# A pre-norm moved behind the projections: x transposed raw, the weights applied at the banks' evacuation, the row factor at the outputs

## Chip, cores, metric

One core of a Trainium2 chip. Times are device microseconds of one execution; the kernel's time is the median of its runs. TensorE is called PE (its weight loads PEld), VectorE DVE, ScalarE ACT, GpSimd POOL, and SP is the engine that issues most transfers.

## What is computed

A decoder layer in float32, 512 tokens of width 2048: RMSNorm, a sparse attention mixer with 16 heads in 4 groups, a residual, RMSNorm, a SwiGLU of width 5632, a residual, the final RMSNorm. What matters here is the first norm and who reads it:

```python
def rmsnorm(x, g):
    x32 = x.astype(jnp.float32)
    y = x32 * lax.rsqrt(jnp.mean(x32 * x32, axis=-1, keepdims=True) + RMS_EPS)
    return (y * g.astype(jnp.float32)).astype(x.dtype)
...
    proj = h @ w_in          # h = rmsnorm(x, mix_norm_g)
    q, kc, vc, ks, vs, kw, vw, gl = jnp.split(proj, bounds, axis=-1)
    q = q.reshape(Bsz, S, G, HPG, DH) * (DH ** -0.5)
    gates = jax.nn.sigmoid(gl.astype(jnp.float32)) ...
```

kc and vc are cut into 31 overlapping blocks and pass a small MLP (compressed keys and values); ks, vs serve the selected branch and kw, vw the window.

## The kernel before

**Precision.** Every float32 operand is split in a high half (a rounding copy on ACT) and a low half (a subtraction on DVE, for some weights on POOL), and each product is three matmuls: high by high, low by high, high by low (`three`, lines 272 to 274 of the kernel before).

**Weights.** A granule is 128 x 1024 elements (512 KB). `Weights` loads granules in one fixed order into three raw buffers (`raw`), splits them into four pairs `whi`, `wlo`, and hands them out: `take` gives the next one and keeps a given number split ahead. The granules in `on_pool` (0, 1 and 3 among them) get their low half on POOL, all others on DVE. `low` holds the granules that stand 48 columns into their buffer instead of at its start.

**The front.** The code is written in the order in which each engine executes it; nothing reorders it. x lies in four tiles of 128 tokens, `x0` to `x3`. The norm's weights are spread over all partitions in `gb` by a transfer. For each tile: ACT squares it with a running sum (`squares`, L374), a chain of one-column steps makes the row factor (`rstd_steps`, L217 to L228), `scaled` multiplies row factor and weights into x (three quarters on DVE, L239, one on ACT and POOL, L241 and L242), `transposed` turns it on PE into four banks (L250), and `his` and `los` write the high and low halves to `hn_h` and `hn_l` (L256, L261), laid out as 16 blocks of the width by 512 tokens.

**The first projection.** `ws(ps, i, g, c0, c1)` multiplies granule i of four (a quarter of the width) with the tokens c0 to c1. For the first 256 columns of kc the tokens are done in halves: `ws(..., 0, 256)` for the four granules, between the transposes of tiles 2 and 3, then `ws(..., 256, 512)` for all four. After it PE transposes the compression's position table (L430) and looks up the relative biases (L434).

**Afterwards.** The other projections follow. `kv_out` copies kc and vc from the bank (ACT), `build_blk` cuts the blocks, `mlp1` and `gelu` are the compression MLP, `k_out`, `q_out` and the end of `vpair` write the split keys, queries and values (`split_from`: ACT high half, DVE low half out of the bank). The attention of one head is interleaved with the projections of later heads by `pump`, a budget of PE time per step. Then come the output projection, the second norm, and the SwiGLU (tiles `f`), about 940 us to the end; there seven products stand for eight. `RESYNC` moves a tile by 32 columns in every fourteenth unit.

`hn_h` and `hn_l` have rows of 576 columns, of which 512 are used, from column 16 on in the mixer and from 0 on later.

Of the kernel before, what the change touches and what calls it, by code (L numbers as in the profile page):

```python
# [10 lines left out]
F32 = mybir.dt.float32  # L11
# [50 lines left out]
class Weights:  # L62


    def __init__(self, nc, raw, conv, specs):
        self.nc, self.raw, self.conv, self.specs = nc, raw, conv, specs
        self.nd = self.ncv = self.nt = 0
        self.r, self.c, self.place, self.on_pool, self.low, self.sums = {}, {}, {}, set(), set(), {}

# [10 lines left out]
    def split(self):  # L80
        i = self.ncv
        self.ncv += 1
        nk, ncol, _ = self.specs[i]
        if i in self.place:
            hi, lo = self.place.pop(i)
        else:
            c0 = 48 if i in self.low else 0
# [5 lines left out]
        self.nc.scalar.activation(hi[:, :n], src, AF.Copy)  # L93
        eng = self.nc.gpsimd if i in self.on_pool else self.nc.vector
        eng.tensor_tensor(lo[:, :n], src, hi[:, :n].bitcast(F32), op=OP.subtract)  # L95
# [20 lines left out]
def granules(w_in, w1k, w1v, w_out, f_in, f_out):  # L116
# [12 lines left out]

    low = set()  # L130
    out = cols(C_KC) + cols(C_KC + 256) + cols(C_VC)
# [12 lines left out]
    for g in range(G):  # L144
        out += cols(512 * g + 256)
        if g + 1 < G:
            c = 128 * (g + 1)
            out += two(C_KS + c, C_KW + c)
            low.update(range(len(out), len(out) + 4))
            out += two(C_VS + c, C_VW + c) + cols(512 * (g + 1))  # L150
    low.update(range(len(out), len(out) + 3 * N_SPILL))
    for cb in range(N_SPILL):
        out += [rows(w_out, 4 * i, 4, 256 * cb, 256) for i in range(3)]
    for cb in (2, 3):
        out += [rows(w_out, 2 * i, 2, 512 * cb, 512) for i in range(6)]
    marks = [len(out)]
    out += [rows(w_out, 12 + 2 * i, 2, 512 * cb, 512) for cb in range(4) for i in range(2)]
    for p in range(N_PLAIN):
        out += [(4, 256, [(0, 256, mat(f_in, 512 * i, 4, ffn_col(p), 256, 2 * DFF))]) for i in range(4)]
    return out, [rows(f_out, 2 * j, 2, 512 * b, 512) for b in range(4) for j in ORDER[b]], marks, low  # L160

# [7 lines left out]
def nsa_block(ctx: ExitStack, tc: tile.TileContext, x, rel_bias, mix_g, ffn_g, fin_g, w_in, w_out,  # L169
# [12 lines left out]
    psx = early.enter_context(tc.tile_pool(name="psx", bufs=2, space=PSUM))  # L182
    specs, specs2, marks, low = granules(w_in, w1k, w1v, w_out, f_in, f_out)
    W = Weights(nc, rawp, convp, specs)
    W.low = low
    W.on_pool.update((0, 1, 3))
# [119 lines left out]
    gates = keep.tile([128, NT, H, 3], F32, name="gates")  # L306
    biasc = keep.tile([128, H, 55], F32, name="biasc")
    kcc_h = keep.tile([128, G, 32], F32R, name="kcc_h")
    kcc_l = keep.tile([128, G, 32], F32R, name="kcc_l")
# [7 lines left out]
    kv_tiles(keep, 0)  # L317

    def k_out(ps, i):

        kv = [k[:, 32:].rearrange("p (t b s) -> p b t s", b=2, s=128) for k in KK[i]]
        return lambda b: split_from(ps[b].rearrange("p (t s) -> p t s", s=128), kv[0][:, b], kv[1][:, b])

# [4 lines left out]
    def q_out(ps, h0):  # L328
        def end(u):
            Q[h0 + u] = tuple(qp.tile([128, S], F32R, name=f"q{n}") for n in "hl")  # L330
            split_from(ps[u], Q[h0 + u][0], Q[h0 + u][1], SCALE)

# [3 lines left out]
    with ExitStack() as st1:  # L336
# [11 lines left out]
        with ExitStack() as st0:  # L348
            xp = st0.enter_context(tc.tile_pool(name="xp", bufs=1))
            xt = [xp.tile([128, D], F32, name=f"x{t}") for t in range(NT)]  # L350
            gb = xp.tile([128, D], F32, name="gb")
            junk = xp.tile([128, 1024], F32, name="junk")
            act(warm, epsc, AF.Sqrt)
            CUT = [(0, 1024, 1536, 2048)] + [(0, 1024, 2048)] * 3
            for t in range(NT):
                for c0, c1 in zip(CUT[t], CUT[t][1:]):
                    nc.sync.dma_start(xt[t][:, c0:c1], x[tok(t), c0:c1])
                if t:
                    W.load()
                else:  # L360
                    for i in range(2):
                        c = slice(1024 * i, 1024 * (i + 1))
                        nc.sync.dma_start(gb[:, c], mix_g[0:1, c].to_broadcast([128, 1024]))
# [3 lines left out]
            oh = xp.tile([NB + 1, UL + 16 * CL], F32, name="oh")  # L367
            dve.memset(relt[NB:NB + 1, :], NEG)
            pool.dma_start(relt[:NB, :], rel_bias)
            pool.dma_start(oh, onehot)  # L370

            def squares(t, i):
                c0, c1 = CUT[t][i:i + 2]
                act(junk[:, :c1 - c0], xt[t][:, c0:c1], AF.Square, accum_out=ss[t][:, i:i + 1])  # L374

            ss = [xp.tile([128, len(CUT[t]) - 1], F32, name=f"ss{t}") for t in range(NT)]
            ys = [xp.tile([128, 1], F32, name=f"y{t}") for t in range(NT)]
            rs = [rstd_steps(ss[t], ys[t]) for t in range(NT)]

            def trs():  # L380
                return [ps1.tile([128, 512], F32, name=n) for n in ("tr", "mlp", "tr", "mlp")]

            for i in range(3):
                squares(0, i)
            run(rs[0])
            scaled(xt[0], ys[0], gb, xt[0], 1)
            for i in range(2):
                squares(1, i)
# [4 lines left out]
            his(p0[2:], 0)  # L393
            W.split()
            p1 = transposed(xt[1], range(4), proj_tiles(4))
            los(p0, 0)
            his(p1, 1)
            for i in range(2):
                squares(2, i)
            los(p1, 1, rs[2])  # L400
            run(rs[2])
            W.split()
            squares(3, 0)
            scaled(xt[2], ys[2], gb, xt[2], 1)
            squares(3, 1)
            ps = proj_tiles()
            gs = [W.take(0)]
            run(ws(ps, 0, gs[0], 0, 256))
            p2 = transposed(xt[2], range(4), trs())
            his(p2, 2)  # L410
            los(p2, 2, rs[3])
            run(rs[3])
            W.split()
            scaled(xt[3], ys[3], gb, xt[3], 1)
            W.split()
            for i in (1, 2):
                gs.append(W.take(0))
                run(ws(ps, i, gs[i], 0, 256))
            p3 = transposed(xt[3], range(4), trs())
            his(p3, 3)  # L420
            los(p3, 3)
            gs.append(W.take(0))
            run(ws(ps, 3, gs[3], 0, 256))
            for i in range(4):
                run(ws(ps, i, gs[i], 256, 512, start=False))
                W.ahead(min(i + 1, 3))
            ps_kc0 = ps
            p = ps1.tile([128, 2, 32], F32, name="tr")
# [29 lines left out]
        def kv_out(ps, g0):  # L458
            return lambda u: act(kvT[:, g0 + u], ps[u], AF.Copy)

# [61 lines left out]
        for i in range(8):  # L522
            g = W.take()
            for t in range(NT):
# [4 lines left out]
                if i == 7:  # L529
                    act(VV[0][0][:, t], ps[t][:, :256], AF.Copy)  # L530
                    act(ge[:, t], ps[t][:, 256:304].rearrange("p (n h) -> p n h", n=3), AF.Exp, scale=-1.0)
                    dve.tensor_tensor(VV[0][1][:, t], ps[t][:, :256], VV[0][0][:, t].bitcast(F32), op=OP.subtract)
            if i == 1:
# [37 lines left out]
    with ExitStack() as st2:  # L571
# [34 lines left out]
        def vpair(g):  # L606
            ps = [p.rearrange("p (t c) -> p t c", t=2) for p in proj2()]
            for i in range(4):
                w = W.take()
                for t in range(NT):  # L610
# [8 lines left out]
                    if i == 3 and t % 2:  # L619
                        b = t // 2  # L620
                        split_from(ps[b], VV[g % 2][0][:, 2 * b:2 * b + 2], VV[g % 2][1][:, 2 * b:2 * b + 2])
            done["n"] += 1
# [186 lines left out]

    n2_hl = [t[:, :, :S] for t in hn_t]  # L810
    resid = ctx.enter_context(ExitStack())
# [23 lines left out]
    with tc.tile_pool(name="n2", bufs=1) as n2:  # L835
        act(warm, epsc, AF.Sqrt)
        gb2 = n2.tile([128, D], F32, name="gb2")
        nc.scalar.dma_start(gb2, ffn_g[0:1, :].to_broadcast([128, D]))
        xn = n2.tile([128, D + 16], F32, name="xn")
        wr_h = n2.tile([128, 6, 1024], F32R, name="wr_h")  # L840
# [545 lines left out]
```

## Time and profile before

| | us |
|---|---|
| median of 3 runs | 2196.51 |
| lowest and highest | 2192.6, 2198.13 |
| profiled execution | 2191.91 |
| its span | 2190.2 |
| PE busy | 2146.6 |

The profile is of one execution, 4.6 us under the median of the three runs. In a row of the timeline stand the start, the length, engine, line, operation, output tile <- input tiles, shapes, and in brackets the idle time before it with what ended it; the tile names of one ring of buffers have no number. A row of waits has the waiting engine and line, whom it waited for, the us in total, how often, and the longest.

### The profile page before, as it was taken

How to read it: one execution, taken by the hardware profiler on the slowest of the kernel's cores; microseconds unless marked ns; L12 is line 12 of the kernel's file. 1: busy time of each engine (PE TensorE's matmuls, PEld its weight loads, DVE VectorE, ACT ScalarE, POOL GpSimd, SP SyncE). 2: the span in 40 equal slices, each digit the busy share in tenths (PEclk: the TensorE clock that was granted, in tenths of full speed). 3: DMA queues.
4: the chain of work that ended last, by engine and by line, in shares of the span. 5: the costliest groups of instructions: out<-in, count | busy, mean ns of one | idle time of the engine just before them, and what ended most of it. 6: DMA issues, size and time to landing. Idle time of an engine off the chain costs nothing.

```text
span 2190.2 us, 37229 instructions
## 1 busy us (share of the span) xinstructions
PE 2146.6 (98%) x15154; PEld 1993.1 (91%) x15154; DVE 1564.2 (71%) x2564; ACT 935.7 (43%) x1447; POOL 121.4 (6%) x140
## 2 busy tenths in 40 slices
PE   6999999999999999999999999999999999999997
PEld 5889898888989888899999999999999888999996
DVE  5455565656645536698888888888888787877776
ACT  5343444544544324344444444344343454544344
POOL 3100000000013012000000000000000000001000
PEclk9999999999999999999999999999999999999999
DMA  5655232232263452244433333443334676878884
GB/s 168 208 142 164 77 97 87 83 96 88 92 211 106 164 178 101 97 145 126 130 121 126 126 118 125 126 135 126 120 122 132 243 280 217 293 273 309 303 302 150
DMA packets 240267, 345.18 MB, mean 158 GB/s; under 512 B 12991, under 2 KB 178911, under 8 KB 238944
## 3 DMA queue, kind: packets, MB, share of 16 engines
q1 hardware_dynamic: 225920, 269.39, 38.4%
q0 software_dynamic: 12880, 70.28, 8.3%
q10 hardware_dynamic: 1296, 3.15, 0.4%
q8 instruction: 118, 1.93, 0.4%
q14 instruction: 53, 0.43, 0.1%
HBM read 299.68 MB, written 48.34 MB: 159 GB/s over the span
## 4 chain that ended last, share of the span: by engine, by line
PE 93%; DVE 3%; DMA 2%; ACT 1%; issue 1%; SPq 0%; POOL 0%; ACTq 0%; DVEq 0%; POOLq 0%
PE f L274 18%; PE f L273 18%; PE f L272 18%; PE proj L272 8%; PE proj L274 8%; PE proj L273 8%; PE pt L739 2%; PE pp L274 1%; PE pp L272 1%; PE pp L273 1%; PE o L274 1%; PE o L273 1%; PE s L272 1%; PE s L274 1%; PE o L272 1%; PE s L273 1%
## 5 line engine op out<-in xcount | busy, mean ns | idle before, releaser
L95 DVE TENSOR_TENSOR wlo<-raw,whi 128x1024 fp32r<-128x1024 f32 (+1 forms) x208 | 252.6, 1217 | 142.9 <-ACT whi L93 141.9
L93 ACT ACTIVATE whi<-raw 128x1024 fp32r<-128x1024 f32 (+1 forms) x226 | 234.4, 1041 | 219.7 <-DVE raw L894 122.4
L894 DVE TENSOR_TENSOR tlo<-tt,thi 128x1536 fp32r<-128x1536 f32 (+2 forms) x134 | 195.9, 1462 | 110.8 <-ACT thi L996 88.7
L272 PE MATMUL f<-hn_h,whi 128*128 128x256 f32 x984 | 271.7, 276 | 0.7 <-ACT E L954 0.7
L273 PE MATMUL f<-hn_l,whi 128*128 128x256 f32 x984 | 271.6, 276 | 0.0
L274 PE MATMUL f<-hn_h,wlo 128*128 128x256 f32 x984 | 271.6, 276 | 0.0
L991 ACT ACTIVATE whi<-raw 128x1024 fp32r<-128x1024 f32 x123 | 126.1, 1057 | 292.4 <-DVE raw L894 282.1
L272 PE MATMUL proj<-hn_h,whi 128*128 128x512 f32 (+1 forms) x544 | 209.8, 386 | 1.0 <-DVE hn_l L261 1.0
L274 PE MATMUL proj<-hn_h,wlo 128*128 128x512 f32 (+1 forms) x544 | 207.1, 381 | 0.0
L273 PE MATMUL proj<-hn_l,whi 128*128 128x512 f32 (+1 forms) x544 | 206.7, 380 | 0.0
L272 PEld LDWEIGHTS f<-hn_h,whi 128*128 128x128 f32 x984 | 184.7, 188 | 1.1 <-ACT E L954 1.1
L274 PEld LDWEIGHTS f<-hn_h,wlo 128*128 128x128 f32 x984 | 184.7, 188 | 0.0
L273 PEld LDWEIGHTS f<-hn_l,whi 128*128 128x128 f32 x984 | 184.7, 188 | 0.0
L996 ACT ACTIVATE thi<-tt 128x1536 fp32r<-128x1536 f32 x82 | 121.8, 1486 | 84.6 <-PE f L273 75.9
L894 DVE TENSOR_TENSOR wlo<-raw,whi 128x1024 fp32r<-128x1024 f32 x123 | 147.0, 1223 | 0.0
L272 PE MATMUL proj<-whi,hn_h 128*128 128x256 f32 (+2 forms) x496 | 146.3, 295 | 0.0
L273 PE MATMUL proj<-wlo,hn_h 128*128 128x256 f32 (+2 forms) x496 | 145.2, 293 | 0.0
L274 PE MATMUL proj<-whi,hn_l 128*128 128x256 f32 (+2 forms) x496 | 145.0, 292 | 0.0
L298 DVE TENSOR_TENSOR ptl<-pt,pth 128x128 fp32r<-128x128 f32 (+3 forms) x128 | 62.5, 488 | 99.0 <-ACT pth L297 98.8
L274 PE MATMUL f<-whi,tlo 128*128 128x512 f32 x320 | 125.0, 391 | 0.7 <-DVE tlo L894 0.6
L273 PE MATMUL f<-wlo,thi 128*128 128x512 f32 x320 | 125.0, 391 | 0.0
L272 PE MATMUL f<-whi,thi 128*128 128x512 f32 x320 | 124.7, 390 | 0.0
(316 smaller groups left out, 6212.6 us busy)
## 6 DMA issues: line engine op xcount, KB each, us to landing
raw<-in_ffn_w_in SPq DMA_DIRECT2D x135, 512.0 KB, 3.5
raw<-in_ffn_w_out SPq DMA_DIRECT2D x88, 512.0 KB, 5.9
raw<-in_nsa_w_in SPq DMA_DIRECT2D x48, 512.0 KB, 3.6
rawx<-in_ffn_w_in SPq DMA_DIRECT2D x41, 512.0 KB, 4.9
rawx<-d_a SPq DMA_DIRECT2D x34, 512.0 KB, 5.1
raw<-in_nsa_w_out SPq DMA_DIRECT2D x32, 512.0 KB, 3.7
raw<-in_nsa_w_in SPq DMA_DIRECT2D x56, 256.0 KB, 3.3
ah<-d_s POOLq DMA_DIRECT2D x16, 896.0 KB, 7.0
```

Source lines behind the costliest of these rows:

```text
L93: self.nc.scalar.activation(hi[:, :n], src, AF.Copy)
L95: eng.tensor_tensor(lo[:, :n], src, hi[:, :n].bitcast(F32), op=OP.subtract)
L272: mm(o, ah, bh, start=start, stop=False, skip_group_check=True)
L273: mm(o, ah, bl, start=False, stop=False, skip_group_check=True)
L274: mm(o, al, bh, start=False, stop=stop, skip_group_check=True)
L298: dve.tensor_tensor(lo, psum_ap, hi.bitcast(F32), op=OP.subtract)
L739: nc.tensor.transpose(pt[rows, 128 * (t - kt):128 * (t - kt + 1)], src, ident)
L894: dve.tensor_tensor(o, a, b, op=OP.subtract)
L991: act(h, r, AF.Copy)
L996: act(h, ttf, AF.Copy)
```

## The change

- x is transposed as it lands, without any scaling. It comes in smaller pieces for the first tile, and pieces of the first two tiles are issued on ACT's queue.
- The norm's weights are loaded as 16 rows of 128 and transposed to one value per partition and block (`gcol`). `gains` multiplies them in while it reads a bank: one DVE product into an SBUF tile (`xe`), ACT's high half from that, DVE's low half from both, issued one step later.
- The squares run later on ACT, beside the first projection. One chain makes all four row factors (`ymul`, and `yneg` with the sign turned). A diagonal of them, multiplied on PE by a tile of ones, gives `ybc`: the factor of each token on every partition.
- Where tokens lie along the free dimension (kc, vc, k, q), DVE multiplies the bank by `ybc` (`normed`, and in `kv_out`), and the split reads the result. Where tokens lie along partitions (v, gates), the factor is the scale of ACT's copy or exponential and the scalar of DVE's operation (`v_out`).
- `hn` loses its padding, and the granules stand at 0, 16, 32 or 48 columns of their buffers; `xn` of the second norm becomes 48 columns longer.

```diff
-    hn_t = [hnp.tile([128, KC, S + 64], F32R, name=f"hn_{x}") for x in "hl"]
-    hn_h, hn_l = (t[:, :, 16:16 + S] for t in hn_t)
+    hn_h, hn_l = hn_t = [hnp.tile([128, KC, S], F32R, name=f"hn_{x}") for x in "hl"]
...
+    def normed(p, scale=1.0):
+        t = keep.tile([128, S], F32, name="yt", bufs=2)
+        dve.scalar_tensor_tensor(t, p, scale, ybc, op0=OP.mult, op1=OP.mult)
+        return t
+    def v_out(p, t, hi, lo):
+        y = ymul[:, t:t + 1]
+        act(hi, p, AF.Copy, scale=y)
+        dve.scalar_tensor_tensor(lo, p, y, hi.bitcast(F32), op0=OP.mult, op1=OP.subtract)
...
+            def gains(t, ps):
+                for k, p in ps:
+                    f = xp.tile([128, 4, 128], F32, name="xe", bufs=3)
+                    dve.tensor_tensor(f, p, gcol[:, k].unsqueeze(2).to_broadcast([128, 4, 128]), op=OP.mult)
+                    h, l = (z[:, k, tok(t)] for z in (hn_h, hn_l))
+                    act(h, f, AF.Copy)
+                    while late:
+                        late.pop()()
+                    late.append(lambda f=f, h=h, l=l: dve.tensor_tensor(l, f, h.bitcast(F32), op=OP.subtract))
+                    yield
...
-            run(rs[0])
-            scaled(xt[0], ys[0], gb, xt[0], 1)
...
             p0 = transposed(xt[0], range(4), trs())
-            run(rs[1])
-            his(p0[:2], 0)
-            scaled(xt[1], ys[1], gb, xt[1], 1)
...
+            p1 = transposed(xt[1], range(4), proj_tiles(4))
+            g0, g1 = gains(0, p0), gains(1, p1)
+            next(g0)
+            next(g0)
             W.split()
+            run(g0)
+            next(g1)
             W.split()
+            next(g1)
             ps = proj_tiles()
             gs = [W.take(0)]
             run(ws(ps, 0, gs[0], 0, 256))
...
             for i in range(4):
                 run(ws(ps, i, gs[i], 256, 512, start=False))
                 W.ahead(min(i + 1, 3))
+                if i < 2:
+                    square(3, i)
+                if i == 2:
+                    dve.tensor_reduce(ytmp, ssq, axis=AX.X, op=OP.add)
...
+                    dve.tensor_tensor(diag, ident.unsqueeze(1).to_broadcast([128, NT, 128]),
+                                      ymul.unsqueeze(2).to_broadcast([128, NT, 128]), op=OP.mult)
+            p = ps1.tile([128, S], F32, name="tr")
+            mm(p, ones, diag.rearrange("p t c -> p (t c)"), start=True, stop=True)
+            act(ybc, p, AF.Copy)
...
         def kv_out(ps, g0):
-            return lambda u: act(kvT[:, g0 + u], ps[u], AF.Copy)
+            return lambda u: dve.tensor_tensor(kvT[:, g0 + u], ps[u], ybc, op=OP.mult)
```

More of the change, by code (lines that the diff above doesn't have):

```diff
@@ L128, in rows @@
         return (nk, n, [(0, n, mat(w, 128 * ch, nk, c0, n, D))])
-    low = set()
+    off = {i: 0 for i in range(4)}
     out = cols(C_KC) + cols(C_KC + 256) + cols(C_VC)
@@ L148, in granules @@
             out += two(C_KS + c, C_KW + c)
-            low.update(range(len(out), len(out) + 4))
+            off.update((len(out) + i, 32) for i in range(4))
             out += two(C_VS + c, C_VW + c) + cols(512 * (g + 1))
-    low.update(range(len(out), len(out) + 3 * N_SPILL))
+    off.update((len(out) + i, 32) for i in range(3 * N_SPILL))
     for cb in range(N_SPILL):
@@ L155, in granules @@
         out += [rows(w_out, 2 * i, 2, 512 * cb, 512) for i in range(6)]
+    off.update((i, 16) for i, x in enumerate(out) if any(x is y for y in mk + mv))
     marks = [len(out)]
     out += [rows(w_out, 12 + 2 * i, 2, 512 * cb, 512) for cb in range(4) for i in range(2)]
+    off.update((len(out) + i, 0) for i in range(4))
     for p in range(N_PLAIN):
         out += [(4, 256, [(0, 256, mat(f_in, 512 * i, 4, ffn_col(p), 256, 2 * DFF))]) for i in range(4)]
-    return out, [rows(f_out, 2 * j, 2, 512 * b, 512) for b in range(4) for j in ORDER[b]], marks, low
+    return out, [rows(f_out, 2 * j, 2, 512 * b, 512) for b in range(4) for j in ORDER[b]], marks, off
 def ffn_col(p):
@@ L307, in nsa_block @@
     biasc = keep.tile([128, H, 55], F32, name="biasc")
+    ybc = keep.tile([128, S], F32, name="ybc")
+    ssq = keep.tile([128, NT, 2], F32, name="ssq")
+    ymul, yneg, ytmp = (keep.tile([128, NT], F32, name=n) for n in ("ymul", "yneg", "ytmp"))
     kcc_h = keep.tile([128, G, 32], F32R, name="kcc_h")
@@ L367, in nsa_block @@
             oh = xp.tile([NB + 1, UL + 16 * CL], F32, name="oh")
+            ones = xp.tile([128, 128], F32, name="ones")
+            dve.memset(ones, 1.0)
             dve.memset(relt[NB:NB + 1, :], NEG)
@@ L370, in nsa_block @@
             pool.dma_start(oh, onehot)
[L372 to L381, printed above, removed]
@@ L383, in nsa_block, with trs @@
-            for i in range(3):
-                squares(0, i)
-            run(rs[0])
-            scaled(xt[0], ys[0], gb, xt[0], 1)
-            for i in range(2):
-                squares(1, i)
+            def trs(n=2):
+                return [ps1.tile([128, 512], F32, name=x) for _ in range(n) for x in ("tr", "mlp")]
+            late = []
+            def gains(t, ps):
[8 more added lines that the diff above has]
+                    yield
@@ L408, in nsa_block @@
             run(ws(ps, 0, gs[0], 0, 256))
+            next(g1)
+            W.split()
+            run(g1)
             p2 = transposed(xt[2], range(4), trs())
[L410 to L415, printed above, removed]
             for i in (1, 2):
@@ L418, in nsa_block @@
                 run(ws(ps, i, gs[i], 0, 256))
-            p3 = transposed(xt[3], range(4), trs())
-            his(p3, 3)
-            los(p3, 3)
+            g2 = gains(2, p2)
+            next(g2)
+            W.split()
+            next(g2)
+            square(0, 0)
+            p3 = transposed(xt[3], range(2), [ps1.tile([128, 512], F32, name="proj") for _ in range(2)])
             gs.append(W.take(0))
             run(ws(ps, 3, gs[3], 0, 256))
+            next(g2)
+            square(0, 1)
+            run(g2)
+            p3 += transposed(xt[3], range(2, 4), trs(1))
+            for i, _ in enumerate(gains(3, p3)):
+                square(1 + i // 2, i % 2)
+            late.pop()()
             for i in range(4):
```

70 lines of the change are left out of this document (38 added, 32 removed).

## The prediction

> **What bounds the kernel now.** I read the page's shares and its slices first, then the busy time by stretch of ten microseconds, then TensorE's waits, and last the timeline of the first 65 us. The page:
>
> ```profile
> span 2190.2 us, 37229 instructions
> ...
> PE 2146.6 (98%) x15154; PEld 1993.1 (91%) x15154; DVE 1564.2 (71%) x2564; ACT 935.7 (43%) x1447; POOL 121.4 (6%) x140
> ...
> PE   6999999999999999999999999999999999999997
> ...
> PE 93%; DVE 3%; DMA 2%; ACT 1%; issue 1%; SPq 0%; POOL 0%; ACTq 0%; DVEq 0%; POOLq 0%
> ```
>
> TensorE (PE) is the bound: 98% busy, 93% of the chain that ended last. Of its 43.6 idle us, the first slice (a 6) holds half. The same by stretches (start:end, length, PE busy, matmuls, clock):
>
> ```profile
> 0.00:10.00 10.00, 0.00 (x0) 1.00 0.73 206
> 10.00:20.00 10.00, 4.32 (x17) 1.00 1.04 353
> 20.00:30.00 10.00, 8.54 (x40) 1.00 0.58 200
> 30.00:40.00 10.00, 7.07 (x37) 0.66 0.18 54
> 40.00:50.00 10.00, 8.76 (x73) 1.00 0.36 106
> ```
>
> 21.3 us of the first 50 are idle, and at 30 to 40 us the granted clock is 0.66. In the slices after the first PE shows 9 nearly throughout. TensorE's waits name the cause:
>
> ```profile
> PE tr L250 <- DVE x L239: 15.1, 3, 11.9
> PE proj L250 <- DVE x L239: 3.3, 2, 3.0
> ...
> PE s L272 <- DVE mx L715: 2.1, 2, 1.4
> PE mlp L250 <- DVE x L239: 1.8, 2, 1.2
> PE proj L272 <- DVE hn_l L261: 1.0, 1, 1.0
> ```
>
> 15.1 + 3.3 + 1.8 + 1.0 = 21.2 us: all four are the norm of x. The transposes wait for x scaled by row factor and weights (L239), and the first projection for the low halves (L261). The change takes exactly this scaling from in front of the transposes.
>
> **The change: the start.** Rows of the timeline for the terms (start, length, engine):
>
> ```profile
> 0.80 1.28 ACT L353 ACT_TABLE_LOAD   x1 [0.80 <-PEq L1370]
> 4.61 1.06 ACT L374 ACTIVATE junk<-x 128x1024 f32<-128x1024 f32 x1 [2.31 <-DMA x<-in_x]
> 11.92 1.09 PE L250 MATMUL tr<-ident,x 128*128 128x128 f32 x4 [11.92 <-DVE x L239]
> 12.80 1.06 PE L250 MATMUL mlp<-ident,x 128*128 128x128 f32 x4
> 20.69 1.05 ACT L93 ACTIVATE whi<-raw 128x1024 fp32r<-128x1024 f32 x1
> 22.06 0.68 DVE L261 TENSOR_TENSOR hn_l<-tr,hn_h 128x512 fp32r<-128x512 f32 x1
> 24.20 0.60 ACT L256 ACTIVATE hn_h<-proj 128x512 fp32r<-128x512 f32 x1 [0.25 <-PE proj L250]
> 25.19 0.58 PE L272 MATMUL proj<-hn_h,whi 128*128 128x256 f32 x1 [1.02 <-DVE hn_l L261]
> 28.66 2.38 POOL L95 TENSOR_TENSOR wlo<-raw,whi 128x1024 fp32r<-128x1024 f32 x1 [4.29 <-ACT whi L93]
> 29.02 2.04 DVE L228 TENSOR_TENSOR y<-y,nt 128x1 f32<-128x1 f32 x1
> GB/s 0 216 272 181 200 284 310 288 310 373 392 390 384 384 393 263 76 278 68 0 0 104 246 0 11 0 5 19 321 10 104 246 0 0 0 0 11 130 225 145
> ```
>
> Removed: per token tile the wait for both squares, some 1.4 us of one-column steps, three scalings on DVE, one on ACT and POOL; and 1 MB of transfer (the norm's weights spread over 128 partitions, now 8 KB). Added per quarter tile: one DVE product out of the bank (f), one high half on ACT (h), one low half on DVE (l).
>
> The first half tile of x landed by 4.61 before; its first quarter is now issued alone, so I take 4.0. The second quarter goes out on ACT's queue behind the table load, which ends at 2.08, some 2 us after the first quarter's issue: 5.9, an estimate. A group of four transposes takes 1.09 us in a cold start and the next follows 0.88 later (11.92, 12.80): groups end at 5.1, 7.0, 7.9, 8.7. The second tile's first half: x tile 0, one weight granule and that half are 2 MB; the slices of 1.5 us in the last row reach 2.2 MB by 10.5 us, with the weights' megabyte in them. So its first group ends by 11.2.
>
> On DVE the order is f0 f1 l0 f2 l1 f3 l2, and the next tile's f0, l3, f1, l0; its last l0 releases the first projection matmul, so 11 operations. f I take at 0.68 (L261 has the same shape, out of a bank as well). f0 ends 5.8, f1 7.7, then l0, f2, l1 9.7, f3 10.4. Now a new wait: l has both inputs in SBUF, where L261 has one. In the two rows at 28.66 and 29.02 a DVE instruction of one column with both inputs in SBUF takes 2.04 us and ends with POOL's split. So I let l2 wait for POOL's low half of granule 0, which starts after ACT's high half (1.05 after 8.3) and after l1: 9.7 to 12.1. Queued behind l2 on DVE are everything to l0 and, through it, PE. l2 12.8, f0 13.5, l3 14.1, f1 14.8, l0 15.5. First projection matmul: 15.6, not 25.19.
>
> [...]
>
> **From the first matmul to the end of the first projection.** More rows:
>
> ```profile
> 29.66 0.28 PE L274 MATMUL proj<-hn_h,wlo 128*128 128x256 f32 x1
> 39.41 1.22 DVE L95 TENSOR_TENSOR wlo<-raw,whi 128x1024 fp32r<-128x1024 f32 x1
> 43.42 0.60 PE L250 MATMUL tr<-ident,x 128*128 128x128 f32 x4
> 60.82 0.28 PE L272 MATMUL proj<-hn_h,whi 128*128 128x256 f32 x1
> 60.94 0.28 PE L273 MATMUL proj<-hn_l,whi 128*128 128x256 f32 x1
> 61.27 0.31 PE L430 MATMUL tr<-ident,pos 32*128 32x32 f32 x2
> 61.50 1.03 PE L434 MATMUL mlp<-oh,relt 33*16 33x512 f32 x2
> 25.64 0.19 ACT L374 ACTIVATION_READ_ACCUMULATOR junk<-x 128x1 f32 x1
> 9.60 0.16 DVE L217 TENSOR_REDUCE ms<-ss 128x1 f32<-128x3 f32 x1 [8.54 <-ACT junk L374]
> 10.86 0.16 DVE L228 TENSOR_TENSOR y<-y,nt 128x1 f32<-128x1 f32 x1
> ```
>
> Before, the projection's last matmul hands over at 61.27. Now, on PE: 24 matmuls from a cold clock 4.3 (25.19 to 29.94 was 4.75, with an interruption), four warm groups of transposes 2.4, 48 matmuls at the step of 0.12 (60.82, 60.94) 5.8, two groups 1.2, 24 matmuls 2.9, two groups 1.2, the 96 of the other tokens 11.5: 29.3 us, so 44.9. DVE stays ahead: after 15.5 it has 21 operations of 0.68, a low half of 1.22 and two more blocks by POOL of up to 2.4, 20.3 us, hence 35.8 or with PE's own pace some 37, while the last low half is needed by about 42.
>
> Then comes a wait that the change adds: one matmul of ones by a diagonal spreads the row factor, and everything on PE stands behind it. It needs all eight squares. The last quarter tiles' first h ends at 30.0 (PE reaches its transposes at 28.1; 0.6 + 0.7 + 0.6). Behind it ACT has three h of 0.6, six squares of 1.25 (1.06 + 0.19) and three high halves of 1.05: 12.5, with a gap of 0.4, so 42.9. DVE's low half 1.22, the factor's chain 1.42 (9.60 to 11.02), its negative 0.2, the diagonal 0.7: 46.4. PE waits 1.5, the matmul takes 1.0 like the pair at 61.50: 47.4. Against 61.27 that is 13.9 us gained.
>
> **Later stages.** Three more rows: PE by stretch (as above), and two groups:
>
> ```profile
> 64.40:113.30 48.90, 48.90 (x217) 1.00 0.70 206
> 894.00:938.50 44.50, 44.50 (x193) 1.00 0.31 102
> 940.00:1727.00 787.00, 786.60 (x6913) 1.00 0.40 127
> L301 DVE SCALAR_TENSOR_TENSOR ql<-proj,qh 128x512 fp32r<-128x512 f32 x16 | 11.1, 691 | 5.9 <-ACT qh L300 5.9
> L465 DVE TENSOR_TENSOR blkf<-kvT,posT 128x496 f32<-128x496 f32 x16 | 15.4, 1006 | 0.0
> ```
>
> Evacuations: 16 q and 8 k tiles get one DVE product more at 0.69 (L301's shape), 8 kv copies move from ACT to DVE: 22 us of DVE between 60 and 730 us, where PE has no slack but DVE does (71% over the span). A bank is free after that one product instead of ACT and DVE in turn, so PE is helped there; q and k come 0.7 us later, well ahead of their use. PE waits of DVE in the mixer are 2.1 us for scores; I take 0.5 more, 0 to 3.
>
> Placement: rows of hn lose their padding and the granules other offsets. From the tiles' addresses in the two programs, the distance modulo 256 bytes between a streamed tile and the weights loaded next goes from 0 to 192 for the 384 matmuls of 256 columns in the first projection and the compression MLP, from 192 to 0 for the 192 of 512 columns at 894 us, and stays 192 in the 6,913. In the trace 256 columns at distance 0 step by 0.12, at 192 by 786.6/6913 = 0.114; 512 columns at 192 by 44.5/192 = 0.232, at 0 by 48.9/216 = 0.226. If distance is the cause, 384 x 0.006 + 192 x 0.006 = 3.5 us go; if not, none. I take 2.0: distance and step go together in these stretches, but only by association.
>
> [...]
>
> **Sum.** -13.9 - 2.0 + 0.5 = -15.4; call it 15.5 with the rounding. The profiled execution took 2191.9 (span 2190.2) and becomes 2176.4. It is 4.6 under the median of the three runs, 2196.5, which becomes **2181**.
>
> **Rivals.**
> - *Front bound by DVE.* f reads the weights with a repeated element. L465, also with a repeated operand but strided as well, takes 1.0 us for 496. With f at 1.0 and each of POOL's three splits on the path, 16 x 0.35 + 2 x 2.4 = 10.4 us more on DVE, of which about 6 reach PE: a gain of 9, 2187. For it: the lock is in the trace. Against: L261 at 0.68 and the 5 us of slack by 42. The same time results if the second quarter of x lands 6 us late.
> - *Slower: the long stage falls out of step.* The 6,913 matmuls of 256 columns at 940 to 1727 us run at 0.114 and the same shape elsewhere at 0.12. If the new placement, or the shifted start, puts that stage on 0.12, it costs 6,913 x 0.006 = 41 us: 2196.5 + 41 - 15.5 = 2222. It decides from 940 us on, and 2,600 such matmuls already outweigh the gain. For it: 0.12 exists for this shape. Against: the distance there stays 192.
> - *Larger gain.* No lock at the start (2.4), no wait for the diagonal (1.5), the whole 1.5 of the steps: 2175.
> - *It does not do what it says.* If x's landing set the pace, nothing would move: 2196. Against: ACT waits for x 2.3 us at 4.61, PE until 11.92.
>
> **How the numbers follow.** This kernel's measurement tells a change of about 0.3%, 6.6 us, from none. Forecast 0.68; DVE-bound 0.14, of which I count 0.10 as faster and 0.04 as same; larger gain 0.06; slower 0.09; nothing moves 0.03. So faster 0.84, same 0.07, slower 0.09. The range goes from the larger gain less the runs' spread below (2173) to the DVE-bound case with the spread above it (2190); the slower rival is left out.
>
> **What would show it.** Right: first transposes at 4 to 5 us, first projection matmul at 14 to 17, the position transposes at 45 to 49 instead of 61.27, one wait of the diagonal's matmul of 1 to 3 us, low halves of 2 us or more only beside POOL; the steps at 894 us 0.226. Wrong: PE idle over 20 us in the first 50, f over 0.9 us, PE waits on yt or q above 3 us in the mixer, or any step over 0.117 between 930 and 1710 us.

## The result, and the profile after

The changed kernel takes 2186.61 us (median, 2183.76 to 2189.94), the kernel before in the same comparison 2196.3: ratio 0.9963, 95% interval 0.9948 to 0.9978, 9.7 us less where I had forecast 15.5. The profiled executions, 2189.94 (span 2188.2) and 2191.91, lie only 2 us apart; what became of the forecast gain is the subject below.

The page of the changed kernel:

```profile
span 2188.2 us, 37255 instructions
...
PE 2150.0 (98%) x15157; PEld 1993.7 (91%) x15157; DVE 1581.9 (72%) x2593; ACT 930.6 (43%) x1437; POOL 113.0 (5%) x136
...
PE   7999999999999999999999999999999999999997
...
PE 93%; DVE 3%; DMA 2%; ACT 1%; issue 1%; SPq 0%; ACTq 0%; DVEq 0%
```

TensorE bounds it as before. Its first 60 us by stretch (start:end, length, PE busy, matmuls, granted clock, DMA share, GB/s):

```profile
0.00:10.00 10.00, 4.36 (x17) 1.00 0.76 235
10.00:20.00 10.00, 5.66 (x30) 1.00 1.05 378
20.00:30.00 10.00, 10.00 (x89) 1.00 0.55 159
30.00:40.00 10.00, 10.00 (x87) 1.00 0.13 44
40.00:50.00 10.00, 8.12 (x49) 0.88 0.53 159
50.00:60.00 10.00, 10.00 (x25) 0.61 0.24 65
```

Idle in the first 50 us is 11.9 us now, 21.3 before. But a new low stands at 50 to 60 us: PE is "busy" throughout with 25 matmuls at a clock of 0.61. TensorE's waits:

```profile
PE tr L414 <- DMA g<-in_mix_norm_g: 4.6, 1, 4.6
PE proj L252 <- DMA x<-in_x: 2.8, 1, 2.8
...
PE tr L470 <- DVE diag L467: 1.9, 1, 1.9
...
PE proj L274 <- ACT whi L94: 1.0, 1, 1.0
PE proj L274 <- ACT hn_h L404: 0.8, 1, 0.8
PE proj L275 <- DVE hn_l L407: 0.8, 1, 0.8
...
PE proj L276 <- DVE wlo L96: 0.5, 1, 0.5
```

The 21.2 us of waiting for the norm are gone; what is left at the start are mostly transfers (4.6 and 2.8), and 0.8 each for the high and low halves. New are the 1.9 of the diagonal and the whi and wlo rows, which belong to 190 us. The timeline at the steps of the forecast:

```profile
4.90 1.11 PE L252 MATMUL tr<-ident,x 128*128 128x128 f32 x4
6.05 0.69 DVE L402 TENSOR_TENSOR xe<-tr,gcol 128x512 f32<-128x512 f32 x1 [1.00 <-PE tr L252]
13.13 2.36 POOL L96 TENSOR_TENSOR wlo<-raw,whi 128x1024 fp32r<-128x1024 f32 x1 [9.37 <-ACT whi L94]
13.60 2.44 DVE L407 TENSOR_TENSOR hn_l<-xe,hn_h 128x512 fp32r<-128x512 f32 x1 [2.78 <-ACT hn_h L404]
17.36 0.38 PE L274 MATMUL proj<-hn_h,whi 128*128 128x256 f32 x1 [0.82 <-ACT hn_h L404]
46.63 1.10 PE L470 MATMUL tr<-diag,ones 128*128 128x512 f32 x2 [1.88 <-DVE diag L467]
47.66 0.42 PE L475 MATMUL tr<-ident,pos 32*128 32x32 f32 x2
48.01 1.89 PE L479 MATMUL mlp<-oh,relt 33*16 33x512 f32 x2
53.56 0.79 PE L274 MATMUL proj<-hn_h,whi 128*128 128x512 f32 x1
```

The position transposes start at 47.66 for 61.27: 13.6 us ahead, 13.9 forecast. Then the 512-column table matmul takes 1.89 (1.03 before), and from the transposes to the next projection it is 5.9 us. In the kernel before it was 3.07, from 61.27 to this row:

```profile
64.34 0.50 PE L272 MATMUL proj<-hn_h,whi 128*128 128x512 f32 x1
```

To compare kernels I use starts of the same matmul in all of them, counted among the split products (high and low halves), which are the same 14592 in each. Stage T runs from the 192nd (last of the first projection) to the 401st: waits, row factor, tables, the next projection. Stage V runs from the 941st to the 1001st: the values and the exponentials. "Half" counts the windows of 3.41 us that the clock records of the trace show at half clock in that stage. Each row is one execution.

| kernel | first split matmul | 192nd | T | half in T | V | half in V | span |
|---|---|---|---|---|---|---|---|
| before | 25.2 | 61.1 | 50.5 | 0 | 11.5 | 0 | 2190.2 |
| changed | 17.4 | 44.5 | 58.4 | 3 | 13.4 | 0 | 2188.2 |
| 1 changed, again | 17.0 | 43.5 | 58.4 | 3 | 13.3 | 0 | 2187.2 |
| 2 row factor after the tables | 16.8 | 43.3 | 53.0 | 1 | 13.9 | 0 | 2180.8 |
| 3 exponential first | 16.9 | 45.3 | 58.3 | 3 | 11.4 | 0 | 2182.4 |
| 4 before, with the new placement | 25.4 | 60.4 | 52.2 | 1 | 11.5 | 0 | 2194.0 |
| 5 wait and tables apart | 17.8 | 44.3 | 56.8 | 2 | 17.7 | 2 | 2187.6 |
| 6 tables spread (mostly ahead of T) | 17.0 | 47.7 | 48.2 | 0 | 15.0 | 1 | 2184.2 |
| 7 no low half on GpSimd | 17.3 | 48.8 | 53.6 | 0 | 14.2 | 0 | 2187.6 |
| 8 first split later | 16.5 | 47.8 | 56.8 | 2 | 14.2 | 0 | 2186.2 |
| 9 tables in two pieces | 17.5 | 46.1 | 51.7 | 0 | 19.5 | 2 | 2188.1 |
| 10 = 9 and 3 | 16.7 | 43.2 | 51.8 | 0 | 11.4 | 0 | 2180.4 |
| 11 = 2 and 3 | 16.6 | 45.0 | 53.0 | 1 | 11.4 | 0 | 2182.9 |

Against before, the changed kernel is 16.6 us ahead at the 192nd matmul, gives 7.8 back in T and 1.9 in V, and stands at -6.9 by 230 us. From there to the end its trace loses 4.9 more, mainly 1.6 at 729 us and 4.2 behind the 10,000th split matmul, with 1.2 gained at 900 us. In the trace of experiment 4, the kernel before at the new addresses, the same two losses are 1.3 and 2.9, and over all twelve traces with the new addresses the last one runs from -0.9 to 4.2. So they tell little of the norm.

Two cautions on the table. The 192nd matmul is not exact to the microsecond: experiments 2 and 11 have the same code up to there and 43.3 and 45.0, because the first 24 split matmuls run partly at half speed in one (0.19 us a step for 0.11). And T ends too early for experiments 6, 9 and 10: from the 401st to the 600th they take 1.5, 0.7 and 1.3 us more than the kernel before, all others 0.1 to 0.3 less.

### The profile page after: what moved, and what is told of

Same layout as the page of the kernel before. It is cut to its first block, busy times and chain, and to the rows that moved or that the text cites. A ratio compares the mean times of both kernels' runs of the same rounds, so it can differ in the third digit from the quotient of the medians.

```text
span 2188.2 us, 37255 instructions
## 1 busy us (share of the span) xinstructions
PE 2150.0 (98%) x15157; PEld 1993.7 (91%) x15157; DVE 1581.9 (72%) x2593; ACT 930.6 (43%) x1437; POOL 113.0 (5%) x136
## 4 chain that ended last, share of the span: by engine, by line
PE 93%; DVE 3%; DMA 2%; ACT 1%; issue 1%; SPq 0%; ACTq 0%; DVEq 0%
PE f L276 18%; PE f L275 18%; PE f L274 18%; PE proj L274 8%; PE proj L276 8%; PE proj L275 8%; PE pt L785 2%; DMA tt<-d_a 1%; PE o L275 1%; PE o L276 1%; PE pp L276 1%; PE pp L275 1%; PE s L274 1%; PE pp L274 1%; PE o L274 1%; PE s L276 1%
```

## The experiments

**1. The changed kernel again**, unedited.

> The changed kernel once more, untouched. Which of its late losses belong to the change? If they do, the second profile shows them again at the same places: +1.84 us at the exponentials (about 187 to 194 us of the span), +1.6 at 729 to 732, +3.4 at 1768 to 1780, and the half-clock window at the end twice as long; the profiled span is then again about 2188. My theory: the front repeats to a few tenths (row-factor matmul at 46.6, wait 1.9, bias-table matmuls 5.9 us for 3.1, exponentials +1.84), and the three later losses move or vanish, so that the span lies anywhere from 2182 to 2189 with the sum of the front and the exponentials fixed at about -7 against the kernel before.

2188.9 us (2185.99 to 2189.21), ratio 0.9967 [0.9955, 0.9979]. T and V repeat to 0.2 us, with the three half-clock windows. The three later losses came again, where I had expected them to move or vanish; the other experiments show all the same that the norm's path doesn't set them. The stretch around 729 us (200 split matmuls from the 3616th) took 31.4 and 31.5 in these two, 29.9 in experiments 2 and 3. The difference goes with one half-clock window: nine of the thirteen traces have a record of 3.41 us there (723.5 in the changed kernel) and take 31.2 to 31.5, experiment 4 among them; the kernel before and experiments 2, 3 and 8 have none and take 29.9. The stretch of 1768 us (11,900th to 12,100th) took 36.5 and 35.6, and from 33.1 to 37.2 over all kernels, in no order with the edits (before 33.1). Neither is counted to a step of the forecast. The tail's low clock came twice as long again (6.83 us, 3.41 in the kernel before), but it stands in experiments 2, 3 and 4 too.

**2. The row factor behind the tables.**

```diff
-            p = ps1.tile([128, S], F32, name="tr")
-            mm(p, ones, diag.rearrange("p t c -> p (t c)"), start=True, stop=True)
-            act(ybc, p, AF.Copy)
             ps_kc0 = ps
...
             pool.dma_start(d_u[:, c0:c0 + SPREAD], ...)
+            p = ps1.tile([128, S], F32, name="tr")
+            mm(p, ones, diag.rearrange("p t c -> p (t c)"), start=True, stop=True)
+            act(ybc, p, AF.Copy)
```

> The row-factor matmul and its copy go behind the position transposes and the bias-table matmuls, which need nothing of the diagonal and so fill the wait. Theory (the 1.9 us wait and, behind it, the clock that falls to 0.61 are what the change's gain lost at the front): the wait goes (-1.9), the granted clock stays 1.00 from 40 to 60 us, the bias-table matmuls take 3.1 us as before, the next projection's first matmuls 0.23 each: -1.9 -4.8 = -6.7, so about 2180 beside the changed kernel's 2186.6. Rival (the 33-row matmuls themselves lower the clock, the wait does not): the clock still falls behind 48 us, and only the wait is saved: -1.9, about 2184.7. Rival (the row factor then comes too late for the first normalised tile, whose readers wait): the next projection's first tile ends late and -1 or less is left.

2182.57 us (2179.71 to 2185.11), ratio 0.9943 [0.993, 0.9956]. T shrinks by 5.3, of 6.7 expected. The wait is gone, yet one half-clock window is left. By stretch, and by the timeline:

```profile
40.00:50.00 10.00, 10.00 (x50) 0.87 0.60 167
50.00:60.00 10.00, 10.00 (x44) 0.96 0.84 205
```

```profile
45.65 0.99 PE L476 MATMUL tr<-oh,relt 33*16 33x496 f32 x2
46.58 1.37 PE L488 MATMUL tr<-diag,ones 128*128 128x512 f32 x2
47.14 1.24 PE L274 MATMUL proj<-hn_h,whi 128*128 128x512 f32 x1
48.17 0.63 PE L275 MATMUL proj<-hn_l,whi 128*128 128x512 f32 x1
```

PE is never idle here, the tables run at full speed (0.99), and the clock halves behind them (0.87 from 40 to 50 us, 0.63 a matmul for 0.39): in this trace it fell behind 33-row matmuls, without any wait. So neither cause alone is the whole: the first rival is right for one of the three windows. The total is 6.3 under the changed kernel's second measurement, 2188.9, taken in the same comparison.

**5. Wait and tables apart:** the next projection's first granule between them.

```diff
             ps_kc0 = ps
+            ps_kc1 = proj_tiles()
+            run(ws(ps_kc1, 0, W.take()))
...
-        ps = proj_tiles()
-        for i in range(4):
+        ps = ps_kc1
+        for i in range(1, 4):
             run(ws(ps, i, W.take(), end=kv_out(ps, 2)))
```

> The next projection's first granule goes between the row-factor matmul and the position transposes with the bias-table matmuls: the 1.9 us wait stays, but matmuls of all 128 rows follow it instead of 33-row ones. Theory A (the clock is lowered for the next window of 3.41 us by a window in which TensorE does little, so wait and 33-row matmuls add up): the wait lowers it for one window at the most (about -1.7 us of work), the later 3.1 us of bias tables perhaps for one more; two windows at the most, not three in a row: 1.5 to 4.8 us under the changed kernel, about 2183. Theory B (the wait alone brings all three half-clock windows): the first granule runs at 0.43 to 0.46 a matmul, and nothing is gained, 2187 to 2189. Theory C (the 33-row matmuls alone): full clock until they come, then the same loss behind them.

2187.44 us (2183.85 to 2192.98), ratio 0.9968 [0.9958, 0.9978]. In T it goes as theory A says: one window behind the wait, one behind the tables, each over after 3.41 us (matmuls of the granule, then behind the tables):

```profile
48.09 0.63 PE L275 MATMUL proj<-hn_l,whi 128*128 128x512 f32 x1
...
51.37 0.40 PE L275 MATMUL proj<-hn_l,whi 128*128 128x512 f32 x1
...
58.47 0.63 PE L275 MATMUL proj<-hn_l,whi 128*128 128x512 f32 x1
...
60.99 0.39 PE L275 MATMUL proj<-hn_l,whi 128*128 128x512 f32 x1
```

In the changed kernel the first window falls on the tables and stretches them (1.89 us for 1.03), and the second and third follow at once: one record of 10.24 us at half clock, against two of 3.41 here. As I read the two traces, that chain is what makes three of one. The total gained nothing all the same: in the trace V cost 4.2 more (below), and the expected 2183 was missed.

**7. No low half on GpSimd** for granules 0, 1 and 3.

```diff
-    W.on_pool.update((0, 1, 3))
```

> Granules 0, 1 and 3 have their low halves on VectorE instead of GpSimd; everything else as in the changed kernel. If GpSimd's low half (2.4 us) and VectorE's subtraction that begins beside it (2.3 to 2.4 instead of 0.68) lock each other out, all VectorE subtractions of the norm now take 0.68, three blocks of 1.7 us go, and VectorE takes on three low halves of 1.23: VectorE's front is about 1.5 us shorter, and the first projection starts up to 1.5 us earlier and ends up to 1.5 earlier: 2185 to 2187. Rival (the transfers of x and of the first granule set the front, VectorE does not): within 0.3 us of the changed kernel, with the 0.68 all the same. Rival (VectorE in the order of the program has the low halves in the way of the norm): later by up to 1.

2190.92 us (2189.05 to 2194.02), ratio 0.9986 [0.9976, 0.9996]: 4 us slower than the changed kernel. VectorE's subtractions of the norm all take 0.68, for 2.44 beside GpSimd's 2.36 in the changed kernel, so the lock is real, but the last rival is right in direction: the first split matmul starts as before (17.3), then in program order the low halves of 1.23 and what waits ahead of them hold up the norm, and PE waits 3.0 for hn_l. The 192nd matmul comes 4.3 later. Only 2.2 of this is there at the second split matmul (20.68 for 18.49). The other 2.1 is the clock behind the wait: two half-clock windows from 19.9 to 26.7, in which the split matmuls step by 0.21 us for 0.12.

```profile
20.68 0.58 PE L274 MATMUL proj<-hn_l,whi 128*128 128x256 f32 x1 [3.02 <-DVE hn_l L406]
```

```profile
20.00:30.00 10.00, 9.32 (x57) 0.66 0.45 133
```

Here the lock was the smaller evil. This run also shows the part of chance in the clock:

```profile
51.06 1.10 PE L469 MATMUL tr<-diag,ones 128*128 128x512 f32 x2 [1.98 <-DVE diag L466]
```

```profile
40.00:50.00 10.00, 9.08 (x81) 1.00 0.42 110
50.00:60.00 10.00, 8.94 (x33) 1.00 0.22 63
```

A wait of 1.98 and the tables behind it, and the clock stays 1.00: T is 53.6, the changed kernel's 58.4 less the 4.7 of the three windows. Here the wait, 49.1 to 51.1, happens to lie across the border of two windows (50.6, in steps of 3.41 us from the 26.7 above).

**8. The first split later.**

```diff
-            next(g0)
-            next(g0)
-            W.split()
             run(g0)
+            W.split()
```

> The first granule's split goes behind the whole first tile's gains, so that ScalarE's copies for groups 2 and 3 are not held from 8.7 to 12.0 us behind a weight transfer. If that hold is on the path, the first projection starts earlier by up to 1.7 us (17.4 to 15.7, the start that I had forecast) and the time falls by as much. Rival (the second tile of x lands at 12.8 us whatever stands ahead of it, and its transposes and gains set the start): the first matmul stays within 0.4 us of 17.4, and nothing is gained.

2186.66 us (2184.69 to 2191.07), ratio 0.9969 [0.996, 0.9978]: no gain. The first split matmul comes 0.8 earlier (16.5), but GpSimd's second low half then meets a subtraction (2.86 us on VectorE at 16.76), PE waits 2.6 for hn_l, and the 192nd is 3.3 later. Of this, too, about 2.2 are the first 24 split matmuls at 0.21 us a step for 0.12. The rival had the total right, for another reason. T, with the code of the changed kernel, is 56.8, with two half-clock windows for three.

**3. The exponential ahead of the low half.**

```diff
-                    v_out(ps[t][:, :256], t, VV[0][0][:, t], VV[0][1][:, t])
+                    y = ymul[:, t:t + 1]
+                    act(VV[0][0][:, t], ps[t][:, :256], AF.Copy, scale=y)
                     act(ge[:, t], ps[t][:, 256:304]..., AF.Exp, scale=yneg[:, t:t + 1])
+                    dve.scalar_tensor_tensor(VV[0][1][:, t], ps[t][:, :256], y, VV[0][0][:, t].bitcast(F32), ...)
```

> The exponential of each bank goes between ScalarE's high half and VectorE's low half, as in the kernel before. Theory (on one bank ScalarE and VectorE take turns, and with the low half ahead of the exponential each turn is 1.22 us for 0.83, so that the next weight's high half starts late): the four turns shrink by about 0.4 each, TensorE's waits for whi and wlo behind 192 us (1.0 and 0.5) go, -1.84 us, about 2184.8 beside the changed kernel's 2186.6. Rival (the loss at 194 us is of the weights' arrival, not of the order): nothing moves, 2186.6. Front and everything behind 200 us as in the changed kernel.

2185.16 us (2181.27 to 2191.17), ratio 0.9957 [0.9941, 0.9972]. V falls from 13.4 to 11.4, the value of before; the total is not told apart from the changed kernel's, as the intervals overlap. The timeline of the changed kernel, ScalarE and VectorE on the banks of v:

```profile
188.88 0.47 ACT L332 ACTIVATE v0h<-proj,ymul 128x256 fp32r<-128x256 f32 x1
189.38 0.48 DVE L333 SCALAR_TENSOR_TENSOR v0l<-proj,ymul,v0h 128x256 fp32r<-128x256 f32 x1 [0.74 <-ACT v0h L332]
189.90 0.30 ACT L576 ACTIVATE ge<-proj,yneg 128x48 f32<-128x48 f32 x1 [0.55 <-DVE v0l L333]
190.10 0.47 ACT L332 ACTIVATE v0h<-proj,ymul 128x256 fp32r<-128x256 f32 x1
...
192.54 2.94 ACT L94 ACTIVATE whi<-raw 128x1024 fp32r<-128x1024 f32 x3
```

and of experiment 3:

```profile
189.07 0.46 ACT L576 ACTIVATE v0h<-proj,ymul 128x256 fp32r<-128x256 f32 x1
...
189.43 0.29 ACT L577 ACTIVATE ge<-proj,yneg 128x48 f32<-128x48 f32 x1
189.61 0.48 ACT L576 ACTIVATE v0h<-proj,ymul 128x256 fp32r<-128x256 f32 x1
...
191.25 2.03 ACT L94 ACTIVATE whi<-raw 128x1024 fp32r<-128x1024 f32 x2
```

With the low half in between, a turn holds ScalarE for 1.22 us (188.88 to 190.10), 0.55 of it waiting; without, 0.54. The weights' high halves stand behind four such turns, and TensorE behind them. All other kernels with the new order lost as much or more: experiments 2 and 5 to 9 have V at 13.9 to 19.5. The three with the exponential first (3, 10 and 11) all have 11.4.

**4. The kernel before with the new placement alone:** padding of the normalised tile out, granules' starts and the second norm's tile moved.

```diff
-    hn_t = [hnp.tile([128, KC, S + 64], F32R, name=f"hn_{x}") for x in "hl"]
-    hn_h, hn_l = (t[:, :, 16:16 + S] for t in hn_t)
+    hn_h, hn_l = hn_t = [hnp.tile([128, KC, S], F32R, name=f"hn_{x}") for x in "hl"]
...
-            c0 = 48 if i in self.low else 0
+            c0 = self.off.get(i, self.at)
```

> The kernel before with only the placement part of the change: no padding in front of the normalised tile, the granules' starts moved, 64 columns more on the second norm's tile. The norm, its order and the row factor stay as before. Theory as predicted (the distance of streamed and weight operands sets the step): 512-column steps at 894 us fall from 0.233 to 0.227 (-1.2), the mixer's 256-column ones from 0.120 to 0.117 (-0.5), the first projection's from 0.120 to 0.118 (-0.2): -2, about 2194.4 beside 2196.4 before (my sum had put -2.0, at most -3.5). Rival (placement is nothing, and the steps differ for what else the change does): 0, steps as before.

2192.59 us (2189.67 to 2195.67), ratio 0.9989 [0.998, 0.9998]: 2.5 less. The 512-column steps, ten matmuls from first to last, in the kernel before:

```profile
904.64 0.39 PE L273 MATMUL pp<-hn_l,whi 128*128 128x512 f32 x1
...
906.74 0.39 PE L273 MATMUL pp<-hn_l,whi 128*128 128x512 f32 x1
```

and in experiment 4:

```profile
905.71 0.39 PE L276 MATMUL pp<-hn_h,wlo 128*128 128x512 f32 x1
...
907.75 0.39 PE L276 MATMUL pp<-hn_h,wlo 128*128 128x512 f32 x1
```

2.10 us over nine steps against 2.04: 0.233 and 0.227, with nothing changed but addresses; all twelve traces with the new addresses have 0.227. So the placement does act, by about the 2 us forecast, of which these steps are 1.2. The first projection's 256-column steps went from 0.120 to 0.113, but that isn't shown to come of the addresses: the changed kernel has 0.118 there, and 0.113 in experiment 1, the same program. So the distance alone doesn't set that step. And T shows a half-clock window behind the tables in a kernel without the new wait: in the kernel before, the border of two windows (62.6) fell into the tables, and it has no such window there.

**6. The tables spread** one at a time between the first projection's matmuls, the row factor behind the next projection's first granule.

```diff
+            tabs = tables()
             for i in range(4):
-                run(ws(ps, i, gs[i], 256, 512, start=False))
+                for j, _ in enumerate(ws(ps, i, gs[i], 256, 512, start=False)):
+                    if i in (1, 2) and j in (1, 4):
+                        next(tabs)
```

> The position transposes and the four bias-table matmuls are put one at a time between the 256-column matmuls of the first projection's upper halves, and the row-factor matmul behind the next projection's first granule: no wait and no stretch of small matmuls is left. If a stretch of 3 us of 33-row matmuls without any wait is what left one half-clock window in the kernel with the row factor behind the bias tables (50 to 60 us at 0.96, 0.63 a matmul at 48 to 50 us), the clock now stays at 1.00 from 20 us on: -1.7 beside that kernel (2182.6), about 2181, and -8 at the end of the bias tables beside the changed kernel. Rival (that window had another cause, such as the time since the start): one window at half clock between 45 and 55 us all the same, about 2182.6. Cost that could show instead: VectorE's four table copies (0.65 each) come ahead of the row factor, which nothing waits for here.

2185.87 us (2181.88 to 2188.47), ratio 0.996 [0.9945, 0.9974]. No half-clock window between 20 and 65 us, as the theory says, but the four interruptions cost 4.4 us (the 192nd matmul at 47.7 for 43.3 in experiment 2), the tables in one piece 3.1. Behind T the later row factor costs 1.5 more, and V was hit by one window: not the 2181 expected.

**9, 10 and 11: the combinations.** In 9 the position transposes and two tables fill the wait, and the other two with the row factor follow the next projection's first granule; 10 adds experiment 3 to it, 11 adds it to experiment 2.

```diff
+            tabs = tables()
+            next(tabs)
+            next(tabs)
+            ps_kc1 = proj_tiles()
+            run(ws(ps_kc1, 0, W.take()))
+            run(tabs)
...
+            p = ps1.tile([128, S], F32, name="tr")
+            mm(p, ones, diag.rearrange("p t c -> p (t c)"), start=True, stop=True)
+            act(ybc, p, AF.Copy)
```

> The stretch of small matmuls in two: position transposes and two bias-table matmuls fill the wait; the next projection's first granule follows; the other two tables and the row-factor matmul come behind it. So far a window of 3.41 us lowered the clock of the next where matmuls of full rows filled less than about 1.4 us of it. Here no window holds more than 1.7 us of 33-row matmuls or waiting in one piece. Theory: no half-clock window between 40 and 65 us whatever the phase, 1.7 better than the kernel with the row factor behind all tables (2182.6): about 2181, and the sixth table-to-projection boundary costs no more than 0.3. Rival (the 33-row matmuls lower the clock even in pieces of 1.5 us): one or two windows at half clock, 2183 to 2185.

> The same, and the exponential ahead of VectorE's low half on each bank. Theory: the two are in different stages and add up: 2181 less 1.3 to 1.8, about 2179.5, the best of these kernels; four v0h-ge turns of 0.54 us at 185 to 190 us. Rival (a stage behind takes the gain back, as the weights' arrival at 190 us): as without it, 2181.

> The row-factor matmul behind all tables, and the exponential ahead of the low half. Theory: 2182.6 less 1.3 to 1.8, about 2181, so 1.5 above the kernel with the tables in two pieces where a half-clock window falls behind the tables, equal where none does. Rival: the pieces make no difference, all three within 1 us.

9: 2184.26 us (2180.2 to 2189.83), ratio 0.995 [0.9936, 0.9963]. 10: 2178.1 (2177.28 to 2182.09), 0.9923 [0.991, 0.9935]. 11: 2181.14 (2176.55 to 2184.64), 0.9934 [0.9922, 0.9947]. In T the pieces keep the clock at 1.00, and T is 51.7 and 51.8, against 53.0 in both kernels with all tables in one stretch. But this gain of 1.3 doesn't last: the row factor now comes later, TensorE waits 0.2 and 0.7 for the blocks of the compression MLP (`blk_l`) just behind T, and 0.2 for a low half. From the 192nd to the 600th matmul experiments 9 and 10 take 1.9 and 2.5 us more than the kernel before, experiments 2 and 11 both 2.2. So in the traces the pieces gained nothing on balance. The last rival had said so, though the three medians don't lie within its 1 us. Experiment 9 lost more in V; its waits and its stretch at 190 us:

```profile
PE proj L274 <- ACT whi L94: 3.8, 1, 3.8
```

```profile
190.00:200.00 10.00, 6.78 (x16) 0.67 0.49 149
```

The late high half leaves PE waiting 3.8 us, and V has two half-clock windows (0.67 from 190 to 200 us). Experiment 10, with the exponential first, at the same places:

```profile
40.00:50.00 10.00, 10.00 (x60) 1.00 0.56 160
50.00:60.00 10.00, 10.00 (x39) 1.00 0.29 76
...
190.00:200.00 10.00, 10.00 (x47) 1.00 0.46 146
```

It beats both kernels: 17 us under before, and its interval lies wholly below the changed kernel's. Whether it beats experiment 11 is open: the intervals overlap, and the traces show no lasting gain of the pieces. 9 alone was expected at 2181 and is not distinguishable from the changed kernel; by the medians the two edits together gave more than their sum. In the traces the order of the exponential also takes away the late high half behind which the clock fell in V.

## Why the prediction was right, and where not

- *The wait for the norm goes:* right. First transposes at 4.90, PE's 21.2 us of waits gone, the position transposes 13.6 earlier for 13.9. The first split matmul came at 17.36, not 15.6, outside the 14 to 17 that I had named: the second tile's transposes began only at 12.86, where I had their first group ended by 11.2, and ScalarE stood from 8.7 to 12.0 behind the first granule. It was made up in the projection.
- *The lock of GpSimd and VectorE:* right, 2.44 us beside 2.36. Beside GpSimd's next low half (18.33 to 20.73) f, out of a bank, kept its 0.68, and the subtraction, from SBUF alone, took 2.32. The rival built on it is out: f takes 0.69, not 1.0, and taking GpSimd out made the kernel slower. So it is luck in part that the time lies in the range: its upper end came from that rival, whose 2187 the kernel hit for another cause. The two bounds don't follow from the spread of the runs either: 2175 less 3.9 is 2171, and 2187 with 1.6 is 2189.
- *The new wait:* 1.88 for 1.5 in length. Here the prediction failed: it charged the wait with its own length and let the tables keep the price of before. I had the granted clock of 0.66 in front of me, for 30 to 40 us of the kernel before, and didn't ask what the new wait would do to it. It costs 4.7 us more (T 58.4 against 53.6 in experiment 7, same wait, full clock). That is no fixed price: of the five traces with this code in T (changed, 1, 3, 7, 8) three have three half-clock windows, one two and one none.
- *Evacuations, +0.5 (0 to 3):* mis-sized. V cost 1.9 and the start of the scores 0.4. I priced the product that was added, not the order on the bank, and the ScalarE queue that has weights behind it. No row of TensorE's waits names the yt tiles.
- *Placement, -2.0:* right in sum, shown alone by experiment 4 (2.5, interval 0.4 to 4.4); of its parts only the step at 900 us is shown. The long stage at 940 us kept its step of 0.113 in both kernels: the slower rival did not come.
- *The sum with measured terms:* -13.6 + 4.7 + 1.9 + 0.4 - 1.7 = -8.3 (the last for the placement behind the tables, 0.5 between T and V, of which experiment 4 has 0.2, and 1.2 at 900 us), against 9.7 between the medians; the interval of the ratio is 4.8 to 11.4 us.

## What to carry to other kernels

A wait that is added to TensorE costs its length and what it does to the clock behind it: here 1.9 us, and 4.7 more in the traces with three half-clock windows. Look what comes next, and put small matmuls into the wait instead of behind it, if they don't need what it waits for: that gave 5.3 us here. Cutting them in pieces as well kept the clock at 1.00 and gained nothing, since what the wait was for came later. When a product moves into the evacuation, write down the order of the engines on one bank and what is queued behind each turn. Executions that differ by a few us may differ by clock windows alone, as T did here by 4.7 us with the same code in it (three windows or none); count them in the trace before a late stage is explained.

## What the runs showed of the hardware

The half-clock records last 3.41 us or multiples of it (6.83 and 10.24 in the two kernels), except the last of a trace, which its end cuts; the full-clock records between them are such multiples too (30.72 us in front of the changed kernel's 10.24). Their phase differs from execution to execution against the kernel's start: in steps of 3.41 us, a border lies 1.20 us behind it in the kernel before and 3.28 in the changed kernel. Experiment 2 lost the clock without a moment of idleness, and the changed kernel after 1.88 us of it. Worked out afterwards from the traces, around the tables, with an estimate of mine from the shapes in the rows above: count a 33-row matmul's time by 33/128 and a full one's whole. Of the windows at full clock with less than 3.2 us of such work, nine were followed by one at half clock and held 1.1 to 1.5 us, and the others held 1.5 to 3.2. The two groups touch at 1.5 (experiment 7 kept its clock behind 1.53, experiment 3 lost it behind 1.54), and no run tested that border by itself.
